# Layer 1's last round of experts: loads and the overflow branch ahead of gate/up, and a fixed order behind

## The chip, the core and the metric

The kernel runs on one core of a Trainium2 chip. The metric is the device time of one execution in microseconds (us). An engine is named as in the profile: PE is TensorE, DVE is VectorE, ACT is ScalarE, POOL is GpSimd and SP is SyncE, which here issues nearly all the DMAs.

## The reference

Two layers act on 256 tokens of 1024 columns (and, in layer 0, on 256 context tokens too). Each has a mixer and then a mixture of experts: 32 experts in 4 groups, of which each token uses two.

```python
def hier_moe(h, w_rg, b_rg, w_re, b_re, w_gate, w_up, w_down):
    ...
    y = jnp.zeros_like(x)
    for g in range(MOE_GROUPS):
        a = jax.nn.silu(jnp.einsum('td,edf->tef', x, w_gate[g])) * jnp.einsum('td,edf->tef', x, w_up[g])
        y = y + jnp.einsum('tef,efd->td', a * comb[:, g, :, None], w_down[g])
    return y.reshape(b_, n, d)
...
        x = x + g1 * o_lat
        x = x + g2 * hier_moe(ada_modulate(x, norm2_g[layer], sh2, sc2), *moe_p)
...
    return rmsnorm(x, final_norm_g)
```

Each expert has three float32 matrices of 1 MB: gate and up (1024 by 256) and down (256 by 1024). In layer 1 only the 256 tokens of x are computed.

## The kernel before, in words

The experts of a layer are worked off in eight rounds (`q` = 0 to 7, the loop of line 1460), four experts to a round, 32 token slots to an expert. A round has these steps, each a method:

- `gather` (line 1615): one-hot matmuls pick the tokens of the round's slots into a tile `X`, ready for the round after.
- `gate_up` (line 1664): 64 matmuls of 32 by 256 on PE, 32 with the gate weights `g` and 32 with the up weights `u`, into one PSUM bank `gu`; then ACT takes the silu (line 1692) and DVE the product with up and the slot weights (line 1693, tile `sge`).
- `turned` (line 1715): two PE transposes of `sge` into PSUM and an ACT copy to `aT`.
- `down` (line 1736): 16 matmuls with the down weights `d` into two PSUM banks `y` (line 1754), one for each half of the 1024 columns, and a product with the gate vector on DVE, giving `z`. In the last round (`last`) the product is `yg` (line 1772), which ACT and DVE split into a high and a low part (lines 172 and 175).
- `selection` (line 1726): POOL makes `esel`, PE multiplies it with the slot table `rqT` (line 1732), DVE compares, giving the 0/1 matrix `sc` that sends slots back to tokens.
- `scatter` (line 1780): four matmuls of `sc` with `z`, and four DVE additions onto the residual `x` (line 1793). The last two rounds add in PSUM instead: four banks `xo` are first loaded with the residual by a product with the identity (line 1758, only if the key `into` is set), and the scatters of rounds 6 and 7 add onto them. `final` (line 1219) normalizes straight from these banks and stores the output.

The rounds are pipelined: in the loop's turn `q` stand gate/up of round q, the scatter of round q-2, the down product of round q-1, the transposes of round q and the gather for round q+1. A scheduler of the language sets the order of the instructions of an engine within these bounds.

Weights come in over SP's queue, one DMA of 1 MB for each matrix (`fetch`, line 1503), in the order g, u of a round and then d of the round before. The tiles rotate through a ring of buffers (`wm`, `self.slots`); a load waits until its buffer is free and until the load eight places ahead of it has landed, since eight semaphores count the DMAs in turn.

`overfull` (line 1434) is a branch on a count from the router: if an expert has more than 32 tokens, its loop works off the rest. With the given inputs it isn't taken in the execution profiled. It has some thousand instructions, which each engine jumps over by itself (line 1436), and each engine then raises its semaphores by what the skipped part would have counted. SP raises those of the DMAs, and it waits for all its loads before it does. In layer 1 the branch stands in the last turn (line 1477), behind gate/up of round 7 and the loads of d, and ahead of the down product of round 6. `rank_rows` (line 1605) after it makes `rqT` anew.

Of the kernel before, what the change touches and what calls it, by code (L numbers as in the profile page):

```python
# [6 lines left out]
F32 = mybir.dt.float32  # L7
# [8 lines left out]
P = 128  # L16
D = 1024
# [75 lines left out]
class K:  # L93
# [33 lines left out]
    def __init__(self, tc, I, C, out, dbg=None, stop=None):  # L127
        self.tc, self.nc, self.I, self.C, self.out = tc, tc.nc, I, C, out
        self.dbg = dbg or {}
        self.stop = stop  # L130
        self.xring = None
        self.turn = 0

    def open(self, name, side="left", **kw):
        return self.tc.alloc_tile_pool(name=name, bufs=1, side=side, reuse_waits="tile", **kw)
# [1265 lines left out]
    def moe(self, layer):  # L1401
        nc = self.nc
        V = nc.vector
        cap, nt, nq, S = self.CAP, self.nt, self.NQ4, self.S
# [10 lines left out]
        segs = list(range(S))  # L1415
# [6 lines left out]
        def more(rv, q):  # L1422
            self.rank_rows(rv)
            for s in segs:
                X = {}
                self.over = self.px.tile([P, 2, 1024], F32, name="over", tag="yl")
                drain(self.gather(rv, 4 * q, 4, s, X, over=True))
                st = self.quad(q, X, [s], self.load_one)
                self.gate_up(st)
                self.turned(st)  # L1430
                self.down(st, [s])
                self.scatter(st, [s])
# [13 lines left out]
        cur = self.quad(0, self.X, segs, self.load)  # L1446
# [12 lines left out]
        Q = {}  # L1459
        for q in range(nq):  # L1460
            end = q == nq - 1
            if cur is None:
                cur = self.quad(q, self.X, segs[::-1] if end else segs, self.load)
                self.gate_up(cur)
            Q[q], cur = cur, None
            if S > 1 and q % 2 and not end:
                for s in segs:
                    drain(self.gather(self.rv, 4 * q + 4, 8, s, self.X))
            if q > 1:
                self.scatter(Q[q - 2], segs)  # L1470
            if layer and end:
                for n in (q - 1, q):
                    Q[n]["d"] = {j: self.load("d", 4 * n + j) for j in range(4)}
                self.fg = self.wm("fg")[:, :D]
                fg = self.I["final_norm_g"]
                nc.sync.dma_start(self.fg, bass.AP(tensor=fg.tensor, offset=fg.offset, ap=[[0, P], [1, D]]))
                overfull()
                self.rank_rows(self.rv)
                Q[q - 1]["into"] = True
            if q:  # L1480
                self.down(Q[q - 1], segs)
            self.turned(Q[q])
            if S == 1 and not end:
                drain(self.gather(self.rv, 4 * q + 4, 4, 0, self.X))
# [179 lines left out]
    def gate_up(self, st, one=None, between=None):  # L1664
# [47 lines left out]
        for s in segs:  # L1712
            mid(s)

    def turned(self, st):
        segs, layer = st["segs"], self.layer
        aT = st["zt"][:, 256:512].rearrange("p (n j s) -> p n j s", n=1, j=2) if "zt" in st else self.cst.tile([P, 1, 2, P], F32, name="aT", tag="c2") if layer else self.p.tile([P, 2, 2, P], F32, name="aT", tag="aT")
        st["aT"] = {}
        for n, s in enumerate(segs):
            pt = self.ps("aT")  # L1720
            for j in range(2):
                self.nc.tensor.transpose(pt[:, j * P:(j + 1) * P], st["sg"][s].rearrange("p (q j) -> p j q", j=2)[:, j, :], self.ident)  # L1722
            st["aT"][s] = a = aT[:, n]
            self.nc.scalar.copy(a, pt[:, :256].rearrange("p (j s) -> p j s", j=2))  # L1724

    def selection(self, st):
        nc, p, nt, q, last = self.nc, self.p, self.nt, st["q"], st["last"]
        pb = self.ps_ada("bc")
        es = p.tile([P, P], BF16, name="esel", tag="esel")
        nc.gpsimd.tensor_copy(es[0:32].rearrange("p (e r) -> p e r", e=4),  # L1730
                              self.idb[0:32, 4 * q:4 * q + 4].unsqueeze(2).to_broadcast([32, 4, self.CAP]))
        nc.tensor.matmul(pb[:, :nt * P], es[0:32], self.rqT[0:32], start=True, stop=True)  # L1732
        st["sc"] = p.tile([P, nt * P], F32 if self.S == 1 and not last else F32R, name="sc", tag="sc")
        nc.vector.tensor_scalar(st["sc"], pb[:, :nt * P], self.slot, None, op0=ALU.is_equal)

    def down(self, st, segs):
        nc, p, I = self.nc, self.p, self.I
        V, S, A = nc.vector, nc.scalar, nc.tensor
        q, parts, load, last = st["q"], st["parts"], st["load"], st["last"]
        py = {(s, hf): self.ps("y") for s in segs for hf in range(2)}  # L1740
        step = 1 if parts == 2 else 4
        kn = 2 // parts
        for h in range(0, 4, step):
            for k0 in range(0, 2, kn):
                if parts == 2:
                    ws = {h: load("d", 4 * q + h, k0, k0 + kn)}
                else:
                    ws = st["d"] = st.get("d") or {j: load("d", 4 * q + j) for j in range(4)}
                for s in segs:
                    for hf in range(2):  # L1750
                        for k in range(k0, k0 + kn):
                            for j, w in ws.items():
                                r = slice(32 * j, 32 * j + 32)
                                A.matmul(py[s, hf][r, :], st["aT"][s][:, k, r], w[:, k - k0, hf * 512:(hf + 1) * 512], start=k == 0, stop=k == 1)  # L1754
        if "into" in st:
            self.xo = {(n, hf): self.ps("xo") for n in range(2) for hf in range(2)}
            for n, hf in self.xo:
                A.matmul(self.xo[n, hf], self.ident, self.xi(2 + n)[:, hf * 512:hf * 512 + 512], start=True, stop=False)  # L1758
        if last:
            zz = self.wm("z", F32R)  # L1760
            self.yg = self.wm("yg")
# [18 lines left out]
    def scatter(self, st, segs):  # L1780
        nc, last = self.nc, st["last"]
        for s in segs:
            for hf in range(2):
                cs = slice(hf * 512, hf * 512 + 512)
                for n in range(2 * s, 2 * s + 2):
                    i = self.tiles[n]
                    into = last or "into" in st
                    o = self.xo[n, hf] if into else self.ps("sc")
                    zs = st["z"][s, hf]
                    for m, z in enumerate(zs):  # L1790
                        nc.tensor.matmul(o, st["sc"][:, n * P:(n + 1) * P], z, start=m == 0 and not into, stop=m == len(zs) - 1 and (last or not into))  # L1791
                    if not into:
                        nc.vector.tensor_tensor(self.xi(i)[:, cs], o, self.xi(i)[:, cs], op=ALU.add)  # L1793

# [28 lines left out]
```

## Time and profile before

| | |
|---|---|
| median of 3 runs | 1109.28 us (1107.37 to 1111.91) |
| the profiled execution, its own time | 1112.03 us |
| its span in the profile | 1110.2 us |
| mean granted PE clock | 0.95 of full speed |
| busy share of the span: PE, DVE, ACT, POOL | 89%, 48%, 36%, 22% |
| DMA | 296.20 MB, 267 GB/s over the span |

Times in the profile run from the start of the span. The profiled execution's own time is 1.8 us longer than its span. The granted clock is the share of PE's full speed that the chip allowed in a stretch: 1.00 is 2.4 GHz and 0.50 is 1.2 GHz. Layer 1's experts fill the span from some 890 us on.

### The profile page before, as it was taken

To read this page: it belongs to the slowest core of one execution; us is meant where nothing else is said; L and a number is where in the kernel's file an instruction comes from. 1 tells how busy PE (TensorE), PEld (TensorE's weight loads), DVE (VectorE), ACT (ScalarE), POOL (GpSimd) and SP (SyncE) were. 2 spreads that over 40 slices of the span, in tenths; PEclk is the share of its full clock that TensorE was granted. 3 is DMA by queue.
4 is the path that set the end of the run, shared out by engine and by line. 5 is a ranking of instruction groups with operands and counts; after the bars stand their busy time and mean duration, and the time that the engine had idled before them with its cause. 6 is when DMAs were issued, how large, how long until landed. Compare 5 with 4: busy or idle time off the path is not lost. (4 is left out here: it accounts for less than half of the span.)

```text
span 1110.2 us, 21447 instructions
## 1 busy us (share of the span) xinstructions
PE 984.5 (89%) x8935; PEld 616.3 (56%) x8935; DVE 532.1 (48%) x1134; ACT 394.2 (36%) x700; POOL 241.5 (22%) x258
## 2 busy tenths in 40 slices
PE   4999696979898889999999989899999799998866
PEld 2666473757676546565654437567665565444322
DVE  4439877467556714453254483143586624222203
ACT  4345454545555502121211145334665521000002
POOL 2216644344514100000000035444441100000000
PEclk9999798979999899999999999899999899989979
DMA  9974526235451379999989976744276789999991
GB/s 300 307 279 151 191 86 229 96 119 190 121 228 63 148 305 418 418 412 376 401 346 402 362 230 160 253 155 170 76 261 211 303 336 420 420 419 422 420 412 54
DMA packets 99316, 296.20 MB, mean 267 GB/s; under 512 B 23000, under 2 KB 57040, under 8 KB 74496
## 3 DMA queue, kind: packets, MB, share of 16 engines
q1 hardware_dynamic: 97344, 292.64, 70.0%
q8 instruction: 74, 1.21, 0.4%
q10 hardware_dynamic: 1200, 1.26, 0.4%
q0 software_dynamic: 656, 0.74, 0.2%
q14 instruction: 42, 0.34, 0.1%
HBM read 293.50 MB, written 1.11 MB: 265 GB/s over the span
## 5 line engine op out<-in xcount | busy, mean ns | idle before, releaser
L1754 PE MATMUL y<-d,aT 128*32 128x512 f32 x768 | 124.3, 600 | 7.0 <-DVEq L1436 6.7
L1686 PE MATMUL gu<-u,X 128*32 128x256 f32 x1536 | 108.1, 404 | 15.3 <-DMA u<-in_moe_w_up_dram 15.3
L1730 POOL COPY esel<-idb 32x128 bf16<-32x128 bf16 x16 | 4.7, 295 | 451.8 <-PE bc L1732 306.6
L1686 PE MATMUL gu<-g,X 128*32 128x256 f32 x1536 | 98.3, 385 | 5.2 <-DVE rq L1608 4.4
L1686 PEld LDWEIGHTS gu<-u,X 128*32 128x32 f32 x1536 | 58.1, 116 | 59.0 <-DMA u<-in_moe_w_up_dram 20.7
L1692 ACT ACTIVATE sge<-gu 128x256 f32<-128x256 f32 x24 | 9.2, 385 | 225.4 <-PE gu L1686 225.4
L1693 DVE SCALAR_TENSOR_TENSOR sge<-gu,ws,sge 128x256 f32<-128x256 f32 x24 | 11.6, 483 | 135.9 <-ACT sge L1692 135.9
L1686 PEld LDWEIGHTS gu<-g,X 128*32 128x32 f32 x1536 | 51.8, 111 | 44.6 <-issue 12.2
L1754 PEld LDWEIGHTS y<-d,aT 128*32 128x32 f32 x768 | 32.8, 110 | 75.5 <-issue 60.0
L1793 DVE TENSOR_TENSOR x<-sc,x 128x512 f32<-128x512 f32 x88 | 56.5, 686 | 34.3 <-PE sc L1791 34.2
L1641 PE MATMUL xg<-onehot,h2h 128*128 128x128 f32 (+1 forms) x384 | 66.9, 292 | 2.4 <-DVE onehot L1629 1.3
L179 PE MATMUL pt<-hh,wh 128*128 128x512 f32 (+1 forms) x160 | 62.2, 389 | 0.3 <-ACT wh L172 0.2
L181 PE MATMUL pt<-hh,wl 128*128 128x512 f32 (+1 forms) x160 | 60.1, 376 | 1.6 <-DVE wl L175 1.2
L180 PE MATMUL pt<-hl,wh 128*128 128x512 f32 (+1 forms) x160 | 59.9, 374 | 1.6 <-DVE hl L431 1.6
L1641 PEld LDWEIGHTS xg<-onehot,h2h 128*128 128x128 f32 x384 | 55.7, 198 | 10.0 <-issue 7.5
L1647 DVE TENSOR_SCALAR X<-xg,ab 128x128 f32<-128x128 f32 (+1 forms) x60 | 27.8, 472 | 68.6 <-PE xg L1641 42.5
L1791 PE MATMUL sc<-z,sc 128*128 128x512 f32 x176 | 57.0, 462 | 2.8 <-ACT z L172 2.1
L175 POOL TENSOR_TENSOR wl<-wcol,wh 128x512 fp32r<-128x512 f32 (+1 forms) x32 | 41.4, 1298 | 57.8 <-ACT wh L172 57.5
L1645 ACT ACTIVATE X<-xg,ab 128x256 f32<-128x256 f32 (+1 forms) x68 | 34.1, 517 | 53.0 <-PE xg L1641 33.7
L172 ACT CAST z<-yg 128x512 fp32r<-128x512 f32 x34 | 20.9, 622 | 77.1 <-DVE yg L1772 69.3
L1791 PEld LDWEIGHTS sc<-z,sc 128*128 128x128 f32 x176 | 31.2, 188 | 28.1 <-issue 15.4
L172 ACT CAST wh<-wcol 128x512 fp32r<-128x512 f32 (+1 forms) x42 | 25.6, 612 | 47.6 <-PE pt L180 33.5
(400 smaller groups left out, 2040.1 us busy)
## 6 DMA issues: line engine op xcount, KB each, us to landing
g<-in_moe_w_gate_dram SPq DMA_DIRECT2D x64, 1024.0 KB, 14.2
u<-in_moe_w_up_dram SPq DMA_DIRECT2D x64, 1024.0 KB, 12.6
d<-in_moe_w_down_dram SPq DMA_DIRECT2D x64, 1024.0 KB, 12.5
wada<-in_ada_w_dram SPq DMA_DIRECT2D x48, 1024.0 KB, 6.7
wcol<-in_ab_w_in_dram SPq DMA_DIRECT2D x8, 1024.0 KB, 8.7
wcol<-in_cd_w_in_dram SPq DMA_DIRECT2D x5, 1024.0 KB, 14.5
wtok<-in_ab_w_in_dram SPq DMA_DIRECT2D x4, 1024.0 KB, 5.3
wout<-in_ab_w_out_dram SPq DMA_DIRECT2D x4, 1024.0 KB, 9.0
```

Source lines behind the costliest of these rows:

```text
L172: nc.scalar.copy(hi, src)
L175: (el or nc.vector).tensor_tensor(lo, src, hi.bitcast(F32), op=ALU.subtract)
L179: mm(out, lh, rh, start=start, stop=False, **kw)
L180: mm(out, lh, rl, start=False, stop=False, **kw)
L181: mm(out, ll, rh, start=False, stop=stop, **kw)
L1641: nc.tensor.matmul(o, h, r, start=i == 0 and n_ == 0, stop=i == 1 and n_ == len(hs) - 1)
L1645: self.xk[k] = nc.scalar.activation(X[:, k], o, AF.Identity, scale=a2[:, k:k + 1], bias=b2[:, k:k + 1])
L1647: nc.vector.tensor_scalar(X[:, k], o, a2[:, k:k + 1], b2[:, k:k + 1], op0=ALU.mult, op1=ALU.add)
L1686: self.mm = A.matmul(pg[s][32 * j:32 * j + 32, c0:c0 + 256], X[:, k, x0 + 32 * j:x0 + 32 * j + 32], w[:, k - k0, :], start=k == 0 and c0 = ...
L1754: A.matmul(py[s, hf][r, :], st["aT"][s][:, k, r], w[:, k - k0, hf * 512:(hf + 1) * 512], start=k == 0, stop=k == 1)
L1791: nc.tensor.matmul(o, st["sc"][:, n * P:(n + 1) * P], z, start=m == 0 and not into, stop=m == len(zs) - 1 and (last or not into))
L1793: nc.vector.tensor_tensor(self.xi(i)[:, cs], o, self.xi(i)[:, cs], op=ALU.add)
```

## The change

For layer 1 and its last round alone:

- the scatter of round 5 stands first, then all loads that remain (g and u of round 7, d of rounds 6 and 7, the final gain `fg`), then the overflow branch and `rank_rows`, and only then gate/up of round 7;
- the load of the residual into `xo` and the selection of round 6 stand ahead of the down product of round 6 instead of in it and behind it;
- from there on the PE instructions of `down`, `turned`, `selection`, `scatter` and the residual load keep the order in which they are written (`kept`, `mmk`);
- the work tile of the branch, `over`, is one tile of another ring instead of one for each use.

```diff
@@ moe: more
-                self.over = self.px.tile([P, 2, 1024], F32, name="over", tag="yl")
+                if not layer:
+                    self.over = self.px.tile([P, 2, 1024], F32, name="over", tag="yl")
@@ moe: the loop over rounds
             end = q == nq - 1
+            if layer and end:
+                self.scatter(Q[q - 2], segs)
+                pre = {(key, 4 * q + j): self.load(key, 4 * q + j) for key in "gu" for j in range(4)}
+                Q[q - 1]["d"] = {j: self.load("d", 4 * q - 4 + j) for j in range(4)}
+                dl = {j: self.load("d", 4 * q + j) for j in range(4)}
+                self.pre.update(pre)
+                self.fg = self.wm("fg")[:, :D]
+                fg = self.I["final_norm_g"]
+                nc.sync.dma_start(self.fg, bass.AP(tensor=fg.tensor, offset=fg.offset, ap=[[0, P], [1, D]]))
+                self.over = self.xring.tile([P, 2, 1024], F32, name="over", tag="xw", bufs=self.nx)
+                overfull()
+                self.rank_rows(self.rv)
+                self.keep = True
+                Q[q - 1]["into"] = True
             if cur is None:
                 cur = self.quad(q, self.X, segs[::-1] if end else segs, self.load)
                 self.gate_up(cur)
+            if layer and end:
+                cur["d"] = dl
             Q[q], cur = cur, None
...
-            if q > 1:
+            if q > 1 and not (layer and end):
                 self.scatter(Q[q - 2], segs)
             if layer and end:
-                for n in (q - 1, q):
-                    Q[n]["d"] = {j: self.load("d", 4 * n + j) for j in range(4)}
-                self.fg = self.wm("fg")[:, :D]
-                fg = self.I["final_norm_g"]
-                nc.sync.dma_start(self.fg, bass.AP(tensor=fg.tensor, offset=fg.offset, ap=[[0, P], [1, D]]))
-                overfull()
-                self.rank_rows(self.rv)
-                Q[q - 1]["into"] = True
+                Q[q - 1]["py"] = {(0, hf): self.ps("y") for hf in range(2)}
+                self.xo = {(n, hf): self.ps("xo") for hf in range(2) for n in range(2)}
+                for n, hf in self.xo:
+                    self.mmk(self.xo[n, hf], self.ident, self.xi(2 + n)[:, hf * 512:hf * 512 + 512], start=True, stop=False)
+                self.selection(Q[q - 1])
@@ the PE instructions of turned, selection, down, scatter go through these
+    def kept(self, ins):
+        return self.tc.keep_in_program_order(ins) if self.keep else ins
+
+    def mmk(self, *a, **kw):
+        return self.kept(self.nc.tensor.matmul(*a, **kw))
```

PE's instructions around the jump, before. Here `gu` is the bank of gate/up of round 7 with its up weights `u`, `y` that of a down product (weights `d_24` to `d_27` are round 6, `d_28` to `d_31` round 7), and `xo` the four banks that hold the output:

```order
L1686 MATMUL gu<-u_31_13282,X 32x256
L1435 TENSOR_LOAD cmx
L1436 COMPARE_AND_BRANCH
...
L1436 UNCONDITIONAL_BRANCH x2
L1754 MATMUL y<-d_24_13330,aT 32x512
L1754 MATMUL y<-d_25_13332,aT 32x512
...
L1758 MATMUL xo<-x_65,ident 128x512 x4
L1722 MATMUL aT<-ident,sge 128x128 x2
```

and now, where `g_28` is the first gate weight of round 7 and `sc<-z_13174` the scatter of round 5:

```order
L1734 MATMUL sc<-z_13174,sc 128x512 x4
L1437 TENSOR_LOAD cmx
L1438 COMPARE_AND_BRANCH
...
L1438 UNCONDITIONAL_BRANCH x2
L1701 MATMUL gu<-g_28_13246,X 32x256
...
L1701 MATMUL gu<-u_31_13260,X 32x256
L1734 MATMUL xo<-x_65,ident 128x512 x4
L1734 LDWEIGHTS esel
L1734 MATMUL bc<-rqT,esel 128x256
L1734 MATMUL y<-d_24_13262,aT 32x512
```

The jump has moved from behind the last matmul of gate/up to ahead of the first, and the residual load from the middle of round 6's down product to ahead of it. Loads on SP stand in the same order in both kernels, with the jump behind the load of `fg`.

DVE's instructions at the end, before (`sc` is the comparison of the selection, `yg` and the second `z` the product and the low part of the split in round 7):

```order
L1767 TENSOR_TENSOR z_15118<-y,g_11324 128x512 x2
L1734 TENSOR_SCALAR sc<-bc,slot 128x256 x2
L1772 TENSOR_TENSOR yg<-y,g_11324 128x512 x2
L175 TENSOR_TENSOR z<-yg,z 128x512 x2
L1230 TENSOR_TENSOR ssf<-ssf 128x1
```

and now:

```order
L1784 TENSOR_TENSOR z_15117<-y,g_11324 128x512 x2
L1789 TENSOR_TENSOR yg<-y,g_11324 128x512
L176 TENSOR_TENSOR z<-yg,z 128x512
L1789 TENSOR_TENSOR yg<-y,g_11324 128x512
L1755 TENSOR_SCALAR sc<-bc,slot 128x256
L176 TENSOR_TENSOR z<-yg,z 128x512
```

The comparison for round 7 has moved from ahead of the round's products to between its two halves.

## Rows read from the trace of the kernel before

**Rows 1.** The chain that ended last, its first pieces: start us, us, what.

```profile
1076.28 3.63 PE y L1754 x8
1079.91 4.40 PE xo L1758 x8
1084.31 0.23 PE aT L1722 x2
...
1084.70 3.44 PE y L1754 x22
```

**Rows 2.** The page, DMA rate in 40 slices of 27.8 us.

```profile
GB/s 300 307 279 151 191 86 229 96 119 190 121 228 63 148 305 418 418 412 376 401 346 402 362 230 160 253 155 170 76 261 211 303 336 420 420 419 422 420 412 54
```

**Rows 3.** Timeline of SP's queue, the last loads: start us, us from first issue to last.

```profile
1046.80 17.71 SPq L1506 DMA_DIRECT2D d<-in_moe_w_down_dram  x8
1066.66 0.33 SPq L1476 DMA_DIRECT2D fg<-in_final_norm_g_dram  x1
```

**Rows 4.** Line 1436 on SP: ends of its waits for landings, layer 1.

```profile
L1436 SPq EVENT_SEMAPHORE  x1: 17/17/17, 1079.0 to 1079.0; - x1
L1436 SPq EVENT_SEMAPHORE  x1: 17/17/17, 1081.6 to 1081.6; - x1
L1436 SPq EVENT_SEMAPHORE  x1: 17/17/17, 1084.0 to 1084.0; - x1
L1436 SPq EVENT_SEMAPHORE  x5: 17/17/17, 1085.3 to 1085.6; - x5
```

**Rows 5.** Line 1436, both layers: ns min/median/max, first and last start us.

```profile
L1436 POOLq EVENT_SEMAPHORE  x4: 17/17/17, 386.6 to 972.0; - x4
L1436 DVEq EVENT_SEMAPHORE  x4: 21/21/21, 391.6 to 1076.1; - x4
L1436 PEldq EVENT_SEMAPHORE  x4: 51/51/51, 391.9 to 1074.3; - x4
L1436 POOLq COMPARE_BRANCH  x2: 53/54/54, 383.9 to 966.6; - x2
...
L1436 PEldq COMPARE_BRANCH  x2: 3622/4854/6085, 388.2 to 1068.0; - x2
L1436 DVEq COMPARE_BRANCH  x2: 63/68/72, 388.6 to 1070.4; - x2
```

**Rows 6.** Timeline, 1050 to 1077 us: start us, us, work, [idle before, releaser].

```profile
1050.90 3.70 PE L1791 MATMUL sc<-z,sc 128*128 128x512 f32 x8
...
1054.53 3.44 PE L1686 MATMUL gu<-g,X 128*32 128x256 f32 x59
1054.64 0.69 DVE L1793 TENSOR_TENSOR x<-sc,x 128x512 f32<-128x512 f32 x1 [0.17 <-PE sc L1791]
...
1064.16 5.41 PE L1686 MATMUL gu<-u,X 128*32 128x256 f32 x58 [1.41 <-DMA u<-in_moe_w_up_dram]
...
1076.28 3.63 PE L1754 MATMUL y<-d,aT 128*32 128x512 f32 x8 [6.71 <-DVEq L1436]
```

**Rows 7.** Stretches after the jumps: us, then engines' busy time, granted clock, DMA, GB/s.

```profile
1080.00:1081.00 1.00, 1.00 (x2) 0.48 (x3) 0.00 (x0) 0.00 (x0) 0.00 (x0) 0.50 0.98 406
1081.00:1082.00 1.00, 1.00 (x3) 0.38 (x2) 0.00 (x0) 0.00 (x0) 0.00 (x0) 0.78 0.87 360
1082.00:1083.00 1.00, 1.00 (x4) 0.52 (x3) 0.00 (x0) 0.00 (x0) 0.00 (x0) 1.00 0.72 295
...
392.00:396.00 4.00, 3.74 (x44) 2.10 (x48) 1.60 (x5) 0.00 (x0) 0.28 (x1) 0.58 0.72 264
```

**Rows 8.** Timeline, 1090 to 1098 us.

```profile
1090.42 3.70 PE L1791 MATMUL xo<-z,sc 128*128 128x512 f32 x8
...
1094.06 0.28 PE L1732 MATMUL bc<-rqT,esel 32*128 32x256 bf16 x1
...
1094.26 3.66 PE L1754 MATMUL y<-d,aT 128*32 128x512 f32 x28
1094.37 0.48 DVE L1734 TENSOR_SCALAR sc<-bc,slot 128x256 fp32r<-128x256 f32 x1 [5.12 <-PE bc L1732]
```

More of the change, by code (lines that the diff above doesn't have):

```diff
@@ L132, in __init__ @@
         self.turn = 0
+        self.keep = False
     def open(self, name, side="left", **kw):
@@ L1721, in turned @@
             for j in range(2):
-                self.nc.tensor.transpose(pt[:, j * P:(j + 1) * P], st["sg"][s].rearrange("p (q j) -> p j q", j=2)[:, j, :], self.ident)
+                self.kept(self.nc.tensor.transpose(pt[:, j * P:(j + 1) * P], st["sg"][s].rearrange("p (q j) -> p j q", j=2)[:, j, :], self.ident))
             st["aT"][s] = a = aT[:, n]
@@ L1731, in selection @@
                               self.idb[0:32, 4 * q:4 * q + 4].unsqueeze(2).to_broadcast([32, 4, self.CAP]))
-        nc.tensor.matmul(pb[:, :nt * P], es[0:32], self.rqT[0:32], start=True, stop=True)
+        self.mmk(pb[:, :nt * P], es[0:32], self.rqT[0:32], start=True, stop=True)
         st["sc"] = p.tile([P, nt * P], F32 if self.S == 1 and not last else F32R, name="sc", tag="sc")
@@ L1739, in down @@
         q, parts, load, last = st["q"], st["parts"], st["load"], st["last"]
-        py = {(s, hf): self.ps("y") for s in segs for hf in range(2)}
+        py = st.get("py") or {(s, hf): self.ps("y") for s in segs for hf in range(2)}
         step = 1 if parts == 2 else 4
@@ L1753, in down @@
                                 r = slice(32 * j, 32 * j + 32)
[L1754 to L1758, printed above, removed]
+                                self.mmk(py[s, hf][r, :], st["aT"][s][:, k, r], w[:, k - k0, hf * 512:(hf + 1) * 512], start=k == 0, stop=k == 1)
         if last:
@@ L1790, in scatter @@
                     for m, z in enumerate(zs):
-                        nc.tensor.matmul(o, st["sc"][:, n * P:(n + 1) * P], z, start=m == 0 and not into, stop=m == len(zs) - 1 and (last or not into))
+                        self.mmk(o, st["sc"][:, n * P:(n + 1) * P], z, start=m == 0 and not into, stop=m == len(zs) - 1 and (last or not into))
                     if not into:
```

## The prediction

> **What bounds the kernel now.** I read the page first, for the DMA rate. From the slice at some 890 us to the one that ends at 1082 us the DMA engines move 412 to 422 GB/s, more than in any other long stretch [rows 2]: layer 1's experts are a stream of weights, and PE waits for it. SP's queue says when the stream ends. The load of `fg`, the last, is issued at 1066.66 us [rows 3], at which time the load eight places ahead of it has landed, the first `d` of round 6. The waits behind SP's jump end at 1079.0, 1081.6 and 1084.0 us, which are the landings of the last three `d` of round 7, and at 1085.3 us, which is `fg` [rows 4]. From 1066.66 to 1084.0 us lie seven loads, 2.48 us each, so that round 6's last `d` lands at 1066.66 + 3 × 2.48 = 1074.1 us. Nothing after that waits for a weight.
>
> Yet the chain of waits does not begin with a landing. It begins on PE, at 1076.28 us, and runs through the down product of round 6, the residual load and the transposes [rows 1]: from there the end is PE's own work. What held PE is in the timeline: the up product ended at 1064.16 + 5.41 = 1069.57 us, and the next matmul started after 6.71 us of idle time that DVE's sequencer ended [rows 6], in line 1436, the jump over the overflow code. PE's own jump instruction took up to 6085 ns; DVE's started at 1070.4 us and let DVE on at 1076.1 us, 5.7 us later [rows 5]. So each engine needs 5.4 to 6.1 us to get across here (POOL, long before, 972.0 - 966.6 = 5.4 us); in layer 0, with little DMA traffic, it was POOL 2.7 and DVE 3.0 us [rows 5]. The weights of round 6 had been there since 1074.1 us, those of round 7 since 1084.0 us, while round 7's down product ran from 1094.26 to 1097.92 us but for its first pair of matmuls [rows 8]. PE is 10 us behind the stream, and all of that is the jump and the slow clock behind it.
>
> **What the change does, step by step.**
>
> *The loads.* SP issues the same loads in the same order, and their buffers are freed by rounds 5 and 6 as before. SP meets its jump at 1067.0 us as before, with every load issued. I keep the landings: 1084.0 us for the last `d`. They could come later only if a buffer came free later; the scatter and the product that free them run ahead of the jump in both kernels.
>
> *The jump, at its new place.* PE comes to it with the scatter of round 5, 1050.90 to 1054.60 us, and DVE with the last addition, at 1054.64 + 0.69 = 1055.33 us [rows 6]. DVE is last, and at the 5.7 us that it needed before, PE starts gate/up at 1061.1 us. The bounds are layer 0's 2.7 us and PE's 6.1 us [rows 5]; the DMA engines are as full at 1055 us as at 1070 us, so I take the loaded price.
>
> *Gate/up of round 7.* Its gate half took 3.44 us for 59 of 64 records at full clock [rows 6], so 3.73 us a half and 7.5 us in all; its last `u` is there at 1064.16 us [rows 6], before that half begins. The clock is the open price. After the jump of before, it stood at 0.50 until past 1081 us, 5.1 us into PE's work, and at 1.00 from 1082 us [rows 7]; in layer 0 the mean of the four microseconds behind the jump was 0.58 [rows 7]. I take 5.1 us at half speed, 2.6 us lost: gate/up ends at 1061.1 + 7.5 + 2.6 = 1071.2 us, 1.6 us later than before. The ends of this price are nothing (1068.6 us) and half speed throughout (1076.1 us). ACT's silu and DVE's product lie beside the residual load.
>
> *The rest of PE's chain*, at full clock: the residual load is of the shape of a scatter's eight records, 3.70 us [rows 8], to 1074.9; the selection's matmul 0.28 us [rows 8], to 1075.2, when all of round 6's `d` has landed; the down product 3.66 us (28 records, [rows 8]; nearly all of one), to 1078.8; the transposes 0.39 us (1084.31 to 1084.70, [rows 1]), to 1079.2; round 6's scatter 3.70 us, to 1082.9. DVE's products for that scatter lie beside the down product's second half and the transposes. The down product of round 7 then meets the stream: its last `d` lands at 1084.0 us, when only its first matmuls are done. I give it the 3.66 us of [rows 8] from there: it ends at 1087.7 us. Without the stream it would have ended at 1086.6 us, so PE's chain has 1.1 us to spare.
>
> *The tail.* Before, from 1097.92 us to the end of the span at 1110.2 us, it took 12.3 us. It keeps its shape, but DVE's comparison for round 7, 0.48 us [rows 8], was done early before and now stands in DVE's line between the halves of the split, where the last scatter waits for it; I charge 0.3 us, with 0 and 0.5 us as its ends. POOL's jump costs nothing: it is there long before.
>
> **The sum.** 1097.92 - 1087.7 = 10.2 us, less 0.3: **9.9 us off**. The profiled execution's span becomes 1100.3 us and its time 1112.03 - 9.9 = 1102.1 us. That execution lies 2.75 us over the median of the runs, so against 1109.28 us I forecast **1099.4 us**.
>
> **The rivals.**
>
> *PE's chain is late (1103 us).* If gate/up runs wholly at half speed, the chain ends at 1061.1 + 15.0 + 3.70 + 0.28 + 3.66 + 0.39 + 3.70 + 3.66 = 1091.5 us instead of 1087.7, and 3.8 us of the gain go: 1103.2 us. A jump slower than 6.1 us works the same way, past the 1.1 us to spare.
>
> *The stall is not the jump's (1109 us).* If the 6.7 us stem from something that stays behind gate/up, PE starts the down product at 1076.3 us as before and nothing is won. For it speaks a figure. The Trainium skill ("Advanced Engine Details and Errata", Control Flow Timing) gives a compare-and-branch as about 108 ns; by it the jump would be no price at either place, and the sum would be about nothing. The trace disagrees: PE's took up to 6085 ns and DVE needed 5.7 us to get across [rows 5], and in both layers the engines' next work waited for it.
>
> *Slower: the clock stays low (1119 us).* The new stall falls ahead of the longest piece of PE work that is left, 22.9 us at full speed from gate/up to round 7's down product. If the clock stays at 0.50 through all of it, the product ends at 1061.1 + 45.8 = 1106.9 us, 9.0 us later than before, and the tail pays 0.3 us more: 1118.6 us. Every microsecond at the low level costs 0.5 us; with 1084.0 us at full speed it breaks even once the low level lasts some 27 us. Against it: 5.1 us behind the old stall and less than four in layer 0 [rows 7]. The Trainium skill ("TensorE: Matmul & The Clock Gate", Seeing it yourself) says that the throttle has been seen stuck for 50 us and more, and warns that such events may be misread; by that the slow case would hold throughout, and no row here shows it.
>
> *Slower too: the jump is a barrier with SP (1122 us).* SP leaves its jump at 1085.6 us, when all loads have landed [rows 4]. If gate/up waited for that, the chain would end at 1085.6 + 2.6 + 22.9 = 1111.1 us, 13.2 us later than before. Before, however, PE went on at 1076.28 us with SP still in its jump [rows 4, 6], so PE doesn't ask SP.
>
> That the change doesn't do what it says is not open: the built order shows the jump ahead of gate/up.
>
> **How the numbers follow.** The stream sets the end: 0.77. PE's chain late, but a gain of 6 us left: 0.10. No change: 0.07. The low clock: 0.04. The barrier: 0.02. A measurement of this kernel tells 0.5% from no change, 5.5 us; the first two cases are over it, 0.87, less a little for a late chain that is later still: faster 0.86, same 0.08, slower 0.06. The range takes in the forecast, the late chain's 1103.2 us, and some 2 us on each side for the spread of the runs shown (1107.37 to 1111.91 us): 1096.5 to 1105.5 us.
>
> **What would show it.** In the new profile, PE should be idle from some 1054.6 to 1061 us with the jump as the releaser, the granted clock should stand at 0.50 until about 1066 us, gate/up should end near 1071 us, and round 7's down product should wait for its last `d` at 1084 us and end near 1087.7 us. The chain that ended last should begin with that DMA. The forecast is wrong if PE is idle between gate/up and round 6's down product again, if `d` lands later than 1084 us, or if the clock is still 0.50 at 1075 us.

## The result, and the profile after

The changed kernel took 1099.39 us in the median of 4 runs (1096.91 to 1102.97), the kernel before 1110.6 us in the median of 4 (1107.37 to 1115.29). The ratio is 0.9898, 95% interval 0.985 to 0.9946. The forecast was 1099.4 us.

The profiled execution's own time is 1098.11 us and its span 1096.2 us, 14.0 us shorter than the span before. Not all of that is the change's. The scatter of round 5, which nothing of the change precedes, ends at 1050.96 us here and ended at 1054.60 us before [rows 6]: 3.6 us of the difference were there already, and such shifts come from one execution to the next. For what happens in the last round I therefore use a length that such a shift leaves alone: from the landing of the last `d` to the end of the span, called **the remainder** from here on. Before it was 1110.2 - 1084.0 = 26.2 us [rows 4].

The waits in SP's jump, and the jump on the other engines (first and last start us), answer to [rows 4, 5]:

```profile
L1438 SPq EVENT_SEMAPHORE  x3: 17/17/17, 1075.4 to 1080.4; - x3
L1438 DVEq EVENT_SEMAPHORE  x4: 21/21/21, 388.6 to 1057.0; - x4
L1438 PEldq COMPARE_BRANCH  x2: 3802/5011/6220, 385.3 to 1048.5; - x2
L1438 DVEq COMPARE_BRANCH  x2: 63/68/72, 385.6 to 1051.4; - x2
```

The last `d` lands at 1080.4 us, so the remainder is 15.8 us: **10.4 us shorter**. The scatter of round 5 ended 1084.0 - 1054.6 = 29.4 us ahead of that landing before, and 1080.4 - 1050.96 = 29.4 us ahead of it now: the stream of weights is as it was. PE's timeline of the last round (start us, us, work, [idle before, releaser]) answers to [rows 6, 8]:

```profile
1047.26 3.70 PE L1734 MATMUL sc<-z,sc 128*128 128x512 f32 x8
1057.14 1.34 PE L1701 MATMUL gu<-g,X 128*32 128x256 f32 x8 [6.18 <-DVEq L1438]
...
1062.49 3.76 PE L1701 MATMUL gu<-u,X 128*32 128x256 f32 x64
1066.18 3.70 PE L1734 MATMUL xo<-x,ident 128*128 128x512 f32 x8
1069.82 0.28 PE L1734 MATMUL bc<-rqT,esel 32*128 32x256 bf16 x1
1070.02 4.06 PE L1734 MATMUL y<-d,aT 128*32 128x512 f32 x32
1074.01 0.51 PE L1743 MATMUL aT<-ident,sge 128*128 128x128 f32 x2
1074.36 3.60 PE L1734 MATMUL xo<-z,sc 128*128 128x512 f32 x8
1077.88 1.08 PE L1734 MATMUL y<-d,aT 128*32 128x512 f32 x6
1080.40 3.62 PE L1734 MATMUL y<-d,aT 128*32 128x512 f32 x26 [1.44 <-SPq L1438]
...
1085.55 2.10 PE L1734 MATMUL xo<-z,sc 128*128 128x512 f32 x8 [1.32 <-DVE sc L1755]
```

The jump's idle time has moved ahead of gate/up, 6.18 us with DVE's sequencer as the releaser. Nothing is idle between gate/up and the down product of round 6 any more, and round 7's down product now stops for its last weight, 1.44 us. SP stands there as the releaser because its jump waits for the same landing; in e4 below, which has no jump, the same wait of 1.44 us is put down to the DMA of `d`. The chain that ended last (start us, us, what) begins with that landing and no longer, as in [rows 1], with PE's own work of round 6:

```profile
1080.40 1.92 PE y L1734 x13
1082.34 0.70 DVE yg L1789
...
1085.01 0.40 DVE sc L1755
```

The granted clock behind the jump, in stretches as in [rows 7]:

```profile
1054.00:1056.00 2.00, 0.00 (x0) 0.00 (x0) 0.00 (x0) 0.00 (x0) 0.28 (x1) 0.54 1.05 430
1056.00:1060.00 4.00, 2.85 (x30) 2.51 (x34) 0.20 (x1) 0.36 (x1) 0.00 (x0) 0.50 1.01 414
1060.00:1061.00 1.00, 1.00 (x16) 0.99 (x12) 0.00 (x0) 0.00 (x0) 0.00 (x0) 0.52 1.05 418
1061.00:1062.00 1.00, 1.00 (x26) 1.00 (x22) 0.00 (x0) 0.00 (x0) 0.00 (x0) 1.00 0.96 401
```

It fell to its lower level (0.50, 1.2 GHz) while PE was idle and came back at 1061 us, 3.9 us into PE's work.

### The profile page after: what moved, and what is told of

Read it like the earlier page. It is cut to its first block, busy times and chain, and to the rows that moved or that the text cites. A ratio compares the mean times of both kernels' runs of the same rounds, so it can differ in the third digit from the quotient of the medians.

```text
span 1096.2 us, 21446 instructions
## 1 busy us (share of the span) xinstructions
PE 977.2 (89%) x8935; PEld 620.5 (57%) x8935; DVE 531.7 (49%) x1134; ACT 394.0 (36%) x700; POOL 241.6 (22%) x258
## 5 line engine op out<-in xcount | busy, mean ns | idle before, releaser
L1734 PE MATMUL y<-d,aT 128*32 128x512 f32 x768 | 120.8, 596 | 1.4 <-SPq L1438 1.4
L1701 PE MATMUL gu<-u,X 128*32 128x256 f32 x1536 | 103.0, 394 | 11.5 <-DMA u<-in_moe_w_up_dram 11.4
L1701 PE MATMUL gu<-g,X 128*32 128x256 f32 x1536 | 100.6, 395 | 10.8 <-DVEq L1438 6.2
L1701 PEld LDWEIGHTS gu<-g,X 128*32 128x32 f32 x1536 | 55.4, 113 | 49.1 <-issue 19.9
L1662 DVE TENSOR_SCALAR X<-xg,ab 128x128 f32<-128x128 f32 (+1 forms) x60 | 27.8, 471 | 69.5 <-PE xg L1656 43.3
L1734 PEld LDWEIGHTS sc<-z,sc 128*128 128x128 f32 x176 | 31.2, 188 | 28.1 <-issue 15.6
## 6 DMA issues: line engine op xcount, KB each, us to landing
g<-in_moe_w_gate_dram SPq DMA_DIRECT2D x64, 1024.0 KB, 14.1
```

Of the source, the lines that this page charges most:

```text
L1662: nc.vector.tensor_scalar(X[:, k], o, a2[:, k:k + 1], b2[:, k:k + 1], op0=ALU.mult, op1=ALU.add)
L1701: self.mm = A.matmul(pg[s][32 * j:32 * j + 32, c0:c0 + 256], X[:, k, x0 + 32 * j:x0 + 32 * j + 32], w[:, k - k0, :], start=k == 0 and c0 = ...
L1734: return self.kept(self.nc.tensor.matmul(*a, **kw))
```

## What the forecast left open, and the theories

The prediction said that PE was 10 us behind the stream and that "all of that is the jump and the slow clock behind it". By that **theory A**, moving the jump alone should bring nearly all of the gain, and the fixed order little. **Theory B**: the order of PE's instructions is a cause of its own. It has two parts, since the change also puts the residual load and the selection of round 6 early. And beside both stood the question whether the stall is the jump's at all.

The table holds all runs, with the remainder from each kernel's trace. e1 to e4 ran on one chip, e5, e6, e7 and e9 on a second, e10 to e12 on a third, and each ratio is against runs of the kernel before on the same chip. e5 and e6 were run once each, so they stand on their traces alone.

| kernel | jump | PE's order | remainder, us | median us (runs) | ratio to before, 95% |
|---|---|---|---|---|---|
| before | late | scheduler's | 26.2 | 1110.6 (4) | |
| the change | early | fixed | 15.8 | 1099.39 (4) | 0.985 to 0.9946 |
| e1_jump_only | early | scheduler's | 22.0 | 1111.04 (10) | 0.9952 to 0.9993 |
| e2_order_only | late | fixed | 22.6 | 1110.31 (10) | 0.9935 to 0.9978 |
| e3_before_no_jump | none | scheduler's | 18.3 | 1103.97 (4) | 0.9864 to 0.9931 |
| e4_after_no_jump | none | fixed | 16.0 | 1100.55 (4) | 0.9841 to 0.9908 |
| e5_two_jumps | two, early | fixed | 18.8 | 1103.35 (1) | |
| e6_free_order | early | scheduler's, residual load early | 19.1 | 1100.9 (1) | |
| e7_early_sel | early | fixed, last selection early | 15.6 | 1100.97 (9) | 0.9921 to 0.9965 |
| e9_halves_sel | early | as e7, round 7's `d` in halves | | 1098.13 (6) | 0.9884 to 0.993 |
| e10_order_late_xo | early | fixed, residual load late | 18.0 | 1104.72 (10) | 0.9914 to 0.9962 |
| e11_after_again | early | fixed | 15.8 | 1100.86 (6) | 0.9868 to 0.9939 |
| e12_halves_again | early | as e9 | | 1101.22 (6) | 0.9864 to 0.9937 |

The remainder of the changed kernel was 15.8 us in both of its traces, where whole runs of it spread over some 6 us (1096.91 to 1102.97). Whole runs follow the remainders only roughly: by e7's remainder its ratio should be 0.990, and the interval lies just above that. The program ahead of the last round shifts too, `fg` being issued anywhere from 1062.61 us (e6, e7) to 1070.40 us (e1), leaving out the halved loads of e9 and e12, and what shifts it stays open. The landing of the last `d` comes 17.3 to 17.7 us after `fg` is issued wherever both are seen; e3 and e4 have no jump on SP to show it, so I took it from there: 1069.79 + 17.35 = 1087.1 us in e3 and 1065.78 + 17.35 = 1083.1 us in e4.

## The experiments

### Is the stall the jump's?

e4 takes the branch out of the changed kernel, e3 out of the kernel before, and e5 puts it in twice.

```diff
@@ e3 (from before), e4 (from the change)
-                overfull()
                 self.rank_rows(self.rv)
@@ e5 (from the change)
                 overfull()
+                overfull()
                 self.rank_rows(self.rv)
```

> The kernel before, with layer 1's overflow branch left out (the work for a 33rd and later token of an expert in layer 1 is not in it). Theory: no stall and no slow clock behind it, the chain starts at 1069.6 us with 19 us of work: 16.5 to 18 us from the landing of the last d to the end of the span, and a ratio of 0.991 to before. Rival (the stall is not the jump's, something else holds PE there): 24 to 26 us.

> The change with layer 1's overflow branch left out (the same work left out). Theory: the jump is wholly hidden, the last landing and the down product behind it set the end: 15.8 us again within 0.3, and the time of the change. Rival (the jump still costs something at its new place): 13 to 15 us, and up to 2 us faster than the change.

> The change with the overflow branch written twice in a row, so that every engine jumps twice. The change's PE had 1.4 us of idle time ahead of the last d and its own work would have ended round 7's down product 2.5 us earlier without that wait. Theory (5.6 us a jump, hidden up to that slack): gate/up starts 5.6 us later and the end moves by 5.6 - 2.5 = 3.1 us: 18.5 to 19.2 us from the landing of the last d to the end of the span, against 15.8. Rival (a second jump is cheap, the cost lies in waiting for the other engines and not in getting across): 15.8 to 16.5 us.

PE's timeline of e3, from the end of gate/up on:

```profile
1067.28 4.84 PE L1685 MATMUL gu<-u,X 128*32 128x256 f32 x57 [1.86 <-DMA u<-in_moe_w_up_dram]
1071.75 0.59 PE L1753 MATMUL y<-d,aT 128*32 128x512 f32 x1
```

With the jump gone there is no gap behind gate/up, and the remainder falls from 26.2 to 18.3 us, somewhat over what was expected. So the 6.71 us of [rows 6] and the slow clock behind them were the jump's, and taking them out gained 7.9 us. The Trainium skill ("Advanced Engine Details and Errata", Control Flow Timing) gives 108 ns for a compare-and-branch. In the changed kernel PE's took 6220 ns; DVE's own instruction took no more than 72 ns, but DVE got across only 5.6 us after it started. The measurement decides: that figure isn't the price of this jump.

e5's PE, the timeline behind the two jumps, and DVE's sequencer there:

```profile
1065.57 1.34 PE L1702 MATMUL gu<-g,X 128*32 128x256 f32 x8 [13.30 <-DVEq L1438]
...
1085.60 3.64 PE L1735 MATMUL y<-d,aT 128*32 128x512 f32 x32
```

```profile
L1438 DVEq EVENT_SEMAPHORE  x4: 21/21/21, 1058.4 to 1065.4; - x4
...
L1438 DVEq COMPARE_BRANCH  x2: 56/60/63, 1052.7 to 1059.0; - x2
```

The second jump adds 13.30 - 6.18 = 7.1 us of idle time, and 3.0 us of the remainder, as expected. Most of the rest went where the change has room: its two down products wait 2.9 us in all for weights, which are gone here, and round 7's starts 1085.60 - 1082.6 = 3.0 us after the last landing. And e4, with no jump, ends no sooner than the changed kernel, 16.0 against 15.8 us; its round 7 waits for the same weight:

```profile
1063.28 5.72 PE L1700 MATMUL gu<-u,X 128*32 128x256 f32 x58 [1.43 <-DMA u<-in_moe_w_up_dram]
...
1080.63 1.07 PE L1733 MATMUL y<-d,aT 128*32 128x512 f32 x6
1083.13 3.62 PE L1733 MATMUL y<-d,aT 128*32 128x512 f32 x26 [1.44 <-DMA d<-in_moe_w_down_dram]
```

Where the jump has gone is visible too. e4's gate/up waits 0.63 + 1.84 + 1.43 = 3.9 us for up weights, the last of them in the first line, and ends 1083.13 - 1069.00 = 14.1 us ahead of the last landing; the changed kernel's, which waits for none, ends 14.2 us ahead of it. So by the remainder the jump costs nothing any more in the changed kernel: its stall and the slow clock lie wholly beside the stream.

### The jump alone, the order alone

e1 has the loads, round 5's scatter and the jump where the change has them, but the scheduler's order, and the residual load and selection where they were before. e2 has the change but for the jump, which stands behind gate/up as before.

```diff
@@ e1 (from the change)
                 self.rank_rows(self.rv)
-                self.keep = True
                 Q[q - 1]["into"] = True
...
-                for n, hf in self.xo:
-                    self.mmk(self.xo[n, hf], self.ident, ...)
-                self.selection(Q[q - 1])
...
+        if "into" in st:
...
+                A.matmul(self.xo[n, hf], self.ident, ...)
@@ e2 (from the change): the branch behind gate/up
-                overfull()
-                self.rank_rows(self.rv)
-                self.keep = True
-                Q[q - 1]["into"] = True
             if cur is None:
...
                 cur["d"] = dl
+                overfull()
+                self.rank_rows(self.rv)
+                self.keep = True
+                Q[q - 1]["into"] = True
```

> The loads, the scatter of round 5 and the jump stand early as in the change, but PE's order behind it is the scheduler's and the residual load and the selection stay inside and behind round 6's down product, as before. Measure: time from the landing of the last d (the last wait but five of SP's in the jump's line) to the end of the span, 26.2 us before and 15.8 us with the change. Theory (the jump hidden under the stream is most of the gain): PE starts its chain near 1070 us on the clock of before and has the 21.6 us of work that it had before less 2.6 us of slow clock, so round 7's down product ends near 1089 us: 17 to 18.5 us, and a time of some 1101 us, ratio 0.992. Rival (the fixed order gives the gain): 25 to 26 us and no difference from before.

> The change with the jump back behind gate/up of round 7; residual load, selection and fixed order as in the change. Theory: the jump's 6.7 us stand in the open again, PE starts at some 1076.3 us on the clock of before and needs 15.4 us at full speed and 2.6 us of slow clock, since each down product now runs with four row groups side by side (3.66 us) instead of in part one by one: end of round 7's down product at 1094.3 us, 22 to 23 us from the landing of the last d to the end of the span, some 3.6 us faster than before. Rival (the order gives the gain): 15.8 us and 1099 us.

e1 missed what was expected: the remainder is 22.0 us, and the runs are faster by 0.27% only. So theory A falls. The jump's move alone gives 26.2 - 22.0 = 4.2 us of the 10.4, the order alone 26.2 - 22.6 = 3.6 us, as expected of e2. In whole runs the medians differ by 2.7 and 3.4 us. PE's timeline of e1 behind gate/up:

```profile
1076.65 1.45 PE L1727 MATMUL y<-d,aT 128*32 128x512 f32 x3
1078.03 2.84 PE L1772 MATMUL xo<-x,ident 128*128 128x512 f32 x6
1080.80 1.90 PE L1727 MATMUL y<-d,aT 128*32 128x512 f32 x4
...
1083.92 3.65 PE L1727 MATMUL y<-d,aT 128*32 128x512 f32 x24
1087.50 1.98 PE L1727 MATMUL xo<-z,sc 128*128 128x512 f32 x4
1089.42 1.90 PE L1727 MATMUL y<-d,aT 128*32 128x512 f32 x4
1091.25 1.98 PE L1727 MATMUL xo<-z,sc 128*128 128x512 f32 x4
1093.16 3.66 PE L1727 MATMUL y<-d,aT 128*32 128x512 f32 x28
```

The down product of round 7 is in two pieces, with half of the scatter between them. PE's instructions there, in the order built for e1 (matmuls; the trace counts two records for each):

```
L1727 MATMUL xo<-z_15111,sc 128x512 x2
L1727 MATMUL y<-d_28_13270,aT 32x512 x2
L1727 MATMUL xo<-z_15111,sc 128x512 x2
L1727 MATMUL y<-d_29_13272,aT 32x512 x2
L1727 MATMUL y<-d_30_13274,aT 32x512 x2
```

and in the fixed order (e10's lines), in turn over the four experts:

```
L1728 MATMUL xo<-z_15111,sc 128x512 x4
L1728 MATMUL y<-d_28_13270,aT 32x512
L1728 MATMUL y<-d_29_13272,aT 32x512
L1728 MATMUL y<-d_30_13274,aT 32x512
L1728 MATMUL y<-d_31_13276,aT 32x512
```

The matmuls of an expert use 32 of PE's 128 columns (128*32 in the rows), for its 32 slots. Two matmuls of one expert by themselves, four records, take 1.90 us, and eight records of two experts beside each other 1.91 us (e6 below), while all 32 records of a product, eight of each expert, take 3.64 us (e2's rounds 6 and 7 below). So in these traces a piece takes as long as the matmuls of the one expert that has most of them in it. A lone piece saves nothing of the rest: its 28 records still hold all eight of each of the other three experts, and take 3.66 us. So round 7's product costs 1.90 + 3.66 = 5.56 us instead of 3.64 us, before as well, where these four records stood ahead of the scatter in [rows 8]:

```profile
1088.59 1.90 PE L1754 MATMUL y<-d,aT 128*32 128x512 f32 x4 [0.25 <-ACT aT L1724]
```

And e1's round 6, in two lone pieces of 1.9 us and a last one of 3.65 us, takes 7.4 us. PE's timeline of e2, behind gate/up:

```profile
1075.76 0.40 PE L1626 MATMUL rqT<-idb,rq 128*32 128x128 bf16 x2 [7.00 <-DVE rq L1623]
1076.09 5.96 PE L1734 MATMUL xo<-x,ident 128*128 128x512 f32 x8
...
1082.19 3.64 PE L1734 MATMUL y<-d,aT 128*32 128x512 f32 x32
...
1089.62 3.64 PE L1734 MATMUL y<-d,aT 128*32 128x512 f32 x32
```

In e2, with the jump late, the stall of 7.00 us and the slow clock are back (the residual load takes 5.96 us instead of 3.70), but each down product is 3.64 us.

### Which part of the order

e6 is the change without the fixed order; e10 is the change with it, but with the residual load and the selection back behind round 6's down product. With e1 and the change they make a square.

```diff
@@ e6 (from the change)
                 self.rank_rows(self.rv)
-                self.keep = True
@@ e10 (from e1)
                 self.rank_rows(self.rv)
+                self.keep = True
...
-                A.matmul(self.xo[n, hf], self.ident, ...)
+                self.mmk(self.xo[n, hf], self.ident, ...)
```

> The change without the fixed order: early jump, early residual load and selection, but the scheduler orders PE. Theory: the down products run in part one by one, some 3.4 us more for round 6 and 1.9 us more for round 7, of which the wait for the stream hides 2.5 us: 17 to 19 us from the landing of the last d to the end of the span. Rival (the order is worth nothing once the jump is early): 15.8 us within 0.3.

> The changed kernel with the jump early and the fixed order kept, but with the residual load and the selection of round 6 back in and behind round 6's down product. Measured from the landing of the last d to the end of the span; before 26.2 us, the change 15.8, jump alone 22.0, jump with early residual load and selection but free order 19.1. Theory (the order of PE's instructions is worth a term of its own: four row groups side by side and a scatter in one piece): the down product of round 6 now waits for its own last d, 9.9 us ahead of the last one, ends 6.2 us ahead of it, and 3.70 + 0.28 + 0.39 + 3.70 + 3.66 us of PE work follow, so round 7's down product ends 5.5 us after the last d and the tail of 12.2 us ends at 17.7 us. Rival (the gain behind the jump comes from the early residual load and selection, the order adds little): 20 to 22 us, as with the jump alone.

The fixed order is worth 22.0 - 18.0 = 4.0 us with the residual load late and 19.1 - 15.8 = 3.3 us with it early. The early residual load and selection are worth 22.0 - 19.1 = 2.9 us in the scheduler's order and 18.0 - 15.8 = 2.2 us in the fixed one. Both came out near the theory (17.7 us for e10, 17 to 19 us for e6) and away from the rivals. On one chip, e10 took 1104.72 us and the changed kernel (e11) 1100.86 us.

The 4.0 us are not the lone pieces alone. In e10 gate/up ends at 1069.47 us, 14.1 us ahead of the last landing, and in e1 only 10.9 us ahead, with two selections among its matmuls. Behind it PE needs 19.5 us to the end of round 7's product in e10, some 2.3 us of them the waits shown next, and 20.0 us in e1. PE's timeline of e10 says what the 2.2 us are:

```profile
1065.75 3.72 PE L1695 MATMUL gu<-u,X 128*32 128x256 f32 x64
1069.20 1.11 PE L1728 MATMUL y<-d,aT 128*32 128x512 f32 x4
1071.18 1.04 PE L1728 MATMUL y<-d,aT 128*32 128x512 f32 x2 [0.86 <-DMA d<-in_moe_w_down_dram]
1073.67 3.62 PE L1728 MATMUL y<-d,aT 128*32 128x512 f32 x26 [1.45 <-DMA d<-in_moe_w_down_dram]
1077.22 3.70 PE L1728 MATMUL xo<-x,ident 128*128 128x512 f32 x8
```

Gate/up is done before round 6's last `d` is there, and PE stands idle for 0.86 + 1.45 = 2.3 us. In the changed kernel the residual load, which needs no weight, fills that time. e6, in the scheduler's order, has both down products in two pieces, round 6's with two experts in the first:

```profile
1071.00 1.91 PE L1733 MATMUL y<-d,aT 128*32 128x512 f32 x8
...
1078.77 1.90 PE L1733 MATMUL y<-d,aT 128*32 128x512 f32 x4
...
1082.52 3.66 PE L1733 MATMUL y<-d,aT 128*32 128x512 f32 x28
```

### Is there more to be had?

In the changed kernel the last scatter is released by DVE's comparison, line 1755, in the chain above. e7 takes the selection of round 7 ahead of its down product. e9 does so too, and loads round 7's `d` in halves of the columns, so that the first half's product need not wait for the last landing; e12 is e9 again, beside the changed kernel again (e11).

```diff
@@ e7 (from the change)
         self.scatter(Q[nq - 2], segs[::-1])
+        if layer:
+            self.selection(Q[nq - 1])
@@ e9 (from e7)
-                dl = {j: self.load("d", 4 * q + j) for j in range(4)}
+                hv = {(hf, m): self.wm("dh") for hf in range(2) for m in range(2)}
+                for (hf, m), t in hv.items():
+                    for i in range(2):
...
+                                          self.I["moe_w_down"][1, g, j].rearrange("(p k) f -> p k f", k=2)[:, :, hf * 512:hf * 512 + 512])
```

> The change with the selection of round 7 ahead of its down product, while PE waits for the last d. Theory (what stands behind the last landing sets the end): DVE's comparison, 0.48 us, leaves the tail and the last scatter can start when the first half is split: 14.6 to 15.3 us from the last landing to the end of the span. Rival (the comparison is hidden in the tail): 15.8 us.

> As the run with the early selection, and round 7's down weights are loaded by halves of the columns, the first halves of all four experts first, in pieces of 0.5 MB. Theory: behind the last landing only half of the second column half's work is left, 1.7 us of PE instead of 3.6, and the first half's split and squares are done: 11.5 to 13.5 us from the last landing to the end of the span, some 3 us faster than the change. Rival: runs of 2 KB instead of 8 KB slow the stream, the last landing comes 1 us or more later and eats the gain.

> The changed kernel once more, on the chip of the two beside it, for a comparison with them and with the kernel before. Both theories expect 15.8 us from the last landing to the end, and a ratio to the kernel before of 0.985 to 0.993.

> Round 7's down weights in two loads for each expert, by halves of the columns, and the selection of round 7 early, beside the changed kernel on one chip. If the wait for the last d is what sets the end, the first half of the columns can be worked off before the last landing and the end comes up to 1.5 us earlier than the changed kernel's, 0.14%, which the runs may just tell. If PE's chain behind the jump is as late as the stream, it is within 0.1% of it.

e7's remainder is 15.6 us, 0.2 less than the change's, and less of a gain than was expected. The comparison is off the path, but the last scatter now waits for the split instead:

```profile
1085.87 0.49 PE L1736 MATMUL xo<-z,sc 128*128 128x512 f32 x1 [0.88 <-ACT z L173]
1086.60 0.96 PE L1736 MATMUL xo<-z,sc 128*128 128x512 f32 x3 [0.23 <-DVE z L176]
```

The halves change what lands last, so the remainder can't be compared: it is 1096.6 - 1082.3 = 14.3 us in e9, where 11.5 to 13.5 us were expected. The issue of round 6's first `d` stands in all of them. From there to the end of the span it is 53.0 us in e11 (1045.10 to 1098.1), 52.4 us in e9 (1044.15 to 1096.6) and 52.1 us in e12 (1046.88 to 1099.0), against 63.4 us before [rows 3]: 0.6 to 0.9 us less than the change, where e9 was expected to bring some 3 us. The rival of e9 came nearly true: from that issue to the last landing it is 38.1 us with halves (1082.3 us in e9, 1085.0 us in e12) and 37.2 us in e11 (1082.3 us), so the stream ends 0.9 us later. In the timelines, e9's round 7 product doesn't wait at all, and e12's, for 0.38 us, in its second half:

```profile
1080.60 3.65 PE L1742 MATMUL y<-dh,aT 128*32 128x512 f32 x32
```

```profile
1085.05 1.91 PE L1742 MATMUL y<-dh,aT 128*32 128x512 f32 x10 [0.38 <-SPq L1438]
```

PE's chain from the jump on is nearly as late as the stream, so little is left to gain by either. Beside each other on one chip, e12 took 1101.22 us and e11 1100.86 us: no difference that the runs tell. None of these versions is shown to beat the changed kernel.

## Why the prediction was right, and where its reason was not

*The loads.* Right: the last `d` lands 29.4 us behind the scatter of round 5 in both kernels. One reading was off, without effect on the sum: the slice at some 890 us moved 336 GB/s, and the 412 to 422 GB/s begin at some 916 us [rows 2].

*The jump at its new place.* Right: 6.18 us of idle PE in place of the forecast's 6.5, ended by DVE, whose sequencer met the jump at 1051.4 us and let DVE on at 1057.0 us.

*Gate/up.* It took 1066.25 - 1057.14 = 9.1 us, of the forecast's 10.1: the clock was low for 3.9 us of PE's work and not 5.1, which is 0.6 us, and at full speed the two halves take some 7.2 us and not 7.5. In e11 it was low until some 1065.9 us, 5.6 us into the work, and gate/up took 10.0 us. The price of the clock varies around the forecast, and the feared long slow stretch did not come. The Trainium skill ("TensorE: Matmul & The Clock Gate", Seeing it yourself) tells of a throttle stuck for 50 us and more. The longest low stretch around the jump in any of these traces is e5's, some 13.7 us (1055.1 to 1068.8 us), and PE stood idle behind two jumps for the first 10.4 us of it.

*PE's chain.* Right in sum: the forecast gave it 1.1 us to spare against the stream. It had 2.5 us (round 7's product started at 1077.88 us and took 6.14 us with its waits, instead of 3.64), and 0.8 us in e11 (from 1081.49 us on it took 4.45 us).

*The tail.* From the end of round 7's product to the end of the span it took 12.2 us (1084.02 to 1096.2), 12.3 before. The 0.3 us charged for the comparison did not show. The comparison does release the last scatter, but e7, which takes it away, gains 0.2 us only.

*The sum.* 9.9 us forecast, 10.4 us in the remainder, 11.2 us between the medians. That the median came out at 1099.39 us against 1099.4 is luck in the last digits: a fourth run moved the median before from 1109.28 to 1110.6 us, and the runs of the changed kernel spread over 6 us. The rivals fell: gate/up did not run at the low clock throughout, the stall was the jump's (e3, e5), and PE did not wait for SP's jump, which it left some 25 us ahead of SP.

**What failed is the sentence "all of that is the jump and the slow clock behind it".** It compared 10 us of delay with 6.7 us of stall and some 2.6 us of clock, and the sums agreed by chance. Behind gate/up, which ends 14.4 us ahead of the last landing before (1069.57 us) and 14.2 us ahead of it now, PE needed 28.35 us to the end of round 7's product before, and needs 17.8 us now. Four things left its chain: the stall, 6.7 us; the clock, 2.6 us; the separate first pieces of round 6's down product (eight records of two experts in [rows 6], some 1.9 us at full clock, as in e6) and of round 7's, 1.9 us; and some 0.5 us around the selections. That is 13.6 us. About 2.9 us of it came back as waits for weights, 0.4 us in round 6's product (4.06 us instead of 3.64) and 2.5 us in round 7's (6.14 us from first to last). The forecast's total was right because it gave each down product the whole 3.66 us and started from the stream, which holds the fixed order's gain without naming it. Anyone who had taken its reason and moved the jump alone would have got 4.2 us instead of 10.

That the jump alone gives no more than 4.2 us, though its removal (e3) gives 7.9, is visible in gate/up. In e1 it ends only 10.9 us ahead of the last landing (1076.8 against 1087.7 us), in e3 14.8 us ahead (1072.3 against 1087.1 us), and these 3.9 us are about the whole difference of the remainders, 3.7 us. e1's gate/up takes 11.4 us where the changed kernel's takes 9.1: two selections with waits of 0.51 and 0.57 us stand between its matmuls, and the granted clock stood at 0.50 until some 1071 us, 5.7 us into the work. Round 6's product is in three pieces in both e1 and e3, against two before, which takes some 1.9 us off what either of them gains. Why the scheduler chose that order stays open.

## What to carry to other kernels

A delay that equals the sum of the stalls in view isn't yet explained by them: add up the work of the bound engine in that stretch too, at the best duration that the same work has anywhere in the trace, since work that is issued in a bad order hides as busy time. Put a jump over long skipped code where the engine that jumps is ahead of a stream anyway, and fill what is left of the wait with work that needs nothing of the stream. To judge a stage when whole executions shift by microseconds, measure from an event of the stage that the edit doesn't move.

## What the runs showed of the hardware

Jumping over the overflow code took about twice as long beside the stream of weights: DVE needed 3.0 us in layer 0 (385.6 to 388.6 us), with the DMA engines at 11 GB/s, 5.6 us in layer 1 at 413 GB/s, and 5.7 and 6.4 us for the two jumps of e5. The Trainium skill ("Runtime: NRT & Kernel Launch", Instruction fetch mechanics) says that a taken branch out of the fetched pages has to wait for a DMA fetch of its target. The trace agrees that there are such fetches: from 1047 to 1058 us the changed kernel has four loads on the instruction queues, one of 16 KB and three of 8 KB, and e4, without the branch, has none in the same time and one of 16 KB just behind it (1058.1 us). But these loads took no longer beside the stream, some 0.3 us for 8 KB against 0.45 us in layer 0's jump, and 1.1 us for 16 KB against 1.3. So why the jump takes twice as long there stays open; the DMA traffic is not the only thing in which the two places differ.

Matmuls of 32 columns overlap if those of different experts stand next to each other: 32 records of four experts took 3.64 us, eight of two experts 1.91 us, and four of one expert alone 1.90 us, more than half of the first time for an eighth of the work. The Trainium skill ("TensorEngine Tiling (Array Packing)", Key Properties) says that different tiles can work in parallel; the trace agrees, and adds what it costs when the matmuls of one tile stand alone between those of a scatter.
